# Hi and lo probabilities as one moving operand, and output parts summed by DRAM to DRAM transfers

## The chip, the cores and the metric

The kernel runs on one core of one Trainium2 chip. The metric is the device time of one execution in microseconds. TensorE multiplies matrices into PSUM, VectorE (DVE), ScalarE (ACT) and GpSimd (POOL) work on tiles, and SyncE (SP) issues the kernel's DMAs. The profile was taken from one execution; the runs were timed without it.

## What is computed

One layer of a streaming encoder in float32: 1024 frames of 1024 channels. Two attention groups of 8 heads each (64 channels per head) feed one output projection; then follow cross-attention into 256 memory rows and a squared-ReLU MLP. The part that the change touches is the token mixing:

```python
def forgetting_attention(q, k, v, f_logit):
    logf = jax.nn.log_sigmoid(f_logit.astype(jnp.float32))
    c = jnp.cumsum(logf, axis=1).transpose(0, 2, 1)
    for i in range(S // Q_BLOCK):
        ...
        logits = logits + c[:, :, q0:q1, None] - c[:, :, None, :q1]
        p = jax.nn.softmax(logits, axis=-1).astype(v.dtype)
        outs.append(jnp.einsum('bhqk,bkhd->bqhd', p, vb))

y = jnp.concatenate([rmsnorm(y_fox, g_fox_out), rmsnorm(y_chk, g_chk_out)], axis=-1)
x = x + rmsnorm(y @ w_out, g_mix_post)
```

The second group (chunked attention) sees its own chunk of 64 frames and the 8 before it, with a bias by relative position.

## The kernel before

**Precision by halves.** Matmuls run on float32r operands. To keep float32 accuracy each operand is kept as a hi half (rounded to float32r) and a lo half (the rest); a product is three matmuls, hi by hi, hi by lo and lo by hi (`mm3`, L172).

**Stages.** The first 80 us or so normalise the input and project the values of the first group. Then `attention_phase` (L1300) runs all attention together with the projections as filler; a second phase runs the output projection's second half and the memory attention; the MLP follows, written out by hand.

**The order of the work** in the attention phase is computed by a planner that runs when the kernel is built (`Flow`, L56). It holds a clock, a queue for each of VectorE ("V"), ScalarE ("S"), GpSimd ("G") and SP's DMA issues ("D"), and streams of TensorE steps (L1308): values, transposes, scores, side steps, and last the filler. At each moment it takes the first stream whose next step is ready by its own estimates. `flow.put(engine, at, cost, call, then, level)` places an operation with an estimated cost. Tokens (`free`, L235) count the buffers of each tag: `u4` counts free tiles of the large pool (34 tiles of 4 KB per partition, L153), from which the halves of the normalised input `hT` (16 tiles), the values `vs` (8), projected queries and keys, and other things are taken. The result is a fixed order of instructions for each engine; semaphores make each wait for its inputs.

**One head.** Scores of 128 queries are matmuls of up to 512 columns (L500, L501); VectorE adds the bias and keeps the minimum (L504), ScalarE takes the exponential (L513), VectorE the reciprocal of the sum (L515), GpSimd scales the probabilities (L516). In `turn_steps` (L556) TensorE transposes four 128 x 128 blocks of probabilities into a PSUM bank (L573): two key blocks by two query blocks. ScalarE copies them as the hi half `ph` (L582) and VectorE subtracts for the lo half `pl` (L579). A block that lies outside the mask is "dead" and left out: three blocks instead of four.

**Values times probabilities.** In `value_steps` (L588) a stationary tile of values holds 64 columns of hi and 64 of lo values of one head, so that one matmul (L613) gives v_hi·p on PSUM partitions 0 to 63 and v_lo·p on 64 to 127. Each step does four of them, `ph` and `pl` for each of two key blocks:

```python
todo = [(full, ph), (1 - full, ph), (1 - full, pl), (full, pl)]
```

A matmul moves 256 columns (two query blocks), or 128 where a block is dead. A unit is one head and one group of 256 queries; there are 64. At the end of a unit ScalarE copies the bank out (L622, 128 x 256), and SP stores the two partition halves to two DRAM tiles, `od[..][..]["h"]` and `["l"]` (L628).

**The outputs.** `Outputs.one` (L888) loads both halves of an output block of 128 channels by 512 frames (L929) for four blocks at a time, adds them (L920, on GpSimd for the first group and on VectorE for the second), scales and splits the sum (L921, L922) and takes the squares (L924, L899). The output projection of the first group (`mix_steps(0)`) comes at the end of the filler, then the memory values, then the second group's in the next phase.

**The gates.** `forget_gates` (L376) makes the logarithms of the gates; two groups of transposes (L401), two ScalarE copies (L405), a running sum on VectorE over 8 x 1024 (L409) and a store to DRAM (L411), from which each head's bias is loaded (L438). Its rows `ea`, `la`, `ua` live in tiles of the tag `klo`.

Of the kernel before, what the change touches and what calls it, by code (L numbers as in the profile page):

```python
# [14 lines left out]
F32 = mybir.dt.float32  # L15
F32R = mybir.dt.float32r
# [119 lines left out]
def build(ctx, tc, nc, out, t):  # L136
# [16 lines left out]
    def u4(name, shape, dt=F32R):  # L153

        return up.tile(list(shape), dt, tag="u4", bufs=34, name=name)
# [44 lines left out]
    od = [[[dr.tile([P, HT], F32, name=f"od{k}_{h}{m}") for m in "hl"] for h in range(2)] for k in range(KC)]  # L200
# [18 lines left out]
    def bias_rows(part):  # L219

        if part == 0:
# [14 lines left out]
            dict(s=2, tr=2, pv=2, mm=2, sp=5, p=2, klo=4, bias=2, raw=2, w=2, ot=3, u4=6,  # L236
# [139 lines left out]
    def forget_gates():  # L376

        z, e, l, u = [p1.tile([P, TB, 8], F32, tag="fg", bufs=4, name=f"f{n}") for n in "zelu"]
        ea, la, ua = [p1.tile([8, S], F32, tag="klo", bufs=4, name=f"f{n}a") for n in "elu"]
# [27 lines left out]
        def scan():  # L407
            vec.memset(ua, 0.0)
            vec.tensor_tensor_scan(la, ea, ua, 0.0, op0=ALU.add, op1=ALU.add)  # L409
# [146 lines left out]
    def turn_steps():  # L556
        for n, a, g in units:
            for c, (kbs, slots, dead) in enumerate(key_steps(n, g)):
# [8 lines left out]
                ph = p1.tile([P, 4, P], F32R, tag="ph", bufs=2, name=f"ph{nm}")  # L567
                pl = p1.tile([P, 4, P], F32R, tag="pl", bufs=2, name=f"pl{nm}")
# [15 lines left out]
                trs[n, a, g, c] = ph, pl  # L584
# [3 lines left out]
    def value_steps():  # L588
        landed = [all_of(("od", k), 32) for k in range(2)]
        for n, a, g in units:  # L590
# [4 lines left out]
            for c, (kbs, slots, dead) in enumerate(steps):  # L595
                yield (0.48, lambda: there(("t", n, a, g, c), ("v", n, 0), ("v", n, 1))
                       and (c or free["pv"].ready() and free["ot"].ready()))
                if c == 0:
                    free["pv"].take()
                    pv = mm_tile([P, 2, P], f"pv{n}{a}{g}", "pv")  # L600
                ph, pl = trs.pop((n, a, g, c))
                full = 1 if dead == [0] else 0
                todo = [(full, ph), (1 - full, ph), (1 - full, pl), (full, pl)]
                for m, (half, x) in enumerate(todo):
                    kb = kbs[slots[2 * half][0]]
                    if n < 4:
# [6 lines left out]
                    nc.tensor.matmul(pv[:, q0:q0 + k1 - k0, :], v, x[:, k0:k1, :], start=c == 0 and m == 0,  # L613
                                     stop=c + 1 == len(steps) and m == 3, skip_group_check=True)
                free["p"].give(flow.end)

            def leave(pv=pv, kind=kind, nm=f"{n}{a}{g}", a=a, kcol=kcol, g=g, step=1 if kind == "f" else -1):
                box = {}

                def copy():  # L620
                    box["t"] = p1.tile([P, 2, P], F32, tag="ot", bufs=3, name=f"ot{nm}")
                    nc.scalar.activation(box["t"][:, :, ::step], pv, AF.Copy)  # L622

                def store(at):
                    free["pv"].give(at)
                    done = all_of(("ot", nm), 2, lambda end: (free["ot"].give(end), landed["fc".index(kind)](end)))
# [97 lines left out]
    def side_steps():  # L724

        yield 0.87, lambda: flow.now > 10.0 and free["tr"].ready(2)
# [5 lines left out]
        def turned(at):  # L732
            for _ in range(2):
                free["tr"].give(at)
            flow.chain(at, [("V", 3.2, gate_scan), ("D", 0.55, gate_store)],
# [136 lines left out]
    class Outputs:  # L872
# [5 lines left out]
        def pump(self):  # L878
            while self.left:
                th, g = self.left[0]  # L880
                if not (there(("od", g)) and ((th, g) == (0, 0) or there("keys")) and free["u4"].ready(12 if (th, g) == (0, 0) else 9)):
                    break
                self.left.pop(0)
                for _ in range(9):
                    free["u4"].take()
                self.one(th, g)

        def one(self, th, g):  # L888
# [4 lines left out]
            ol = [u4(f"oil{th}{g}{i}", (P, 2, HT), F32) for i in range(2)]  # L893
            eng, add_cost, adder = ("G", 1.45, nc.gpsimd) if g == 0 else ("V", 0.7, nc.vector)
# [3 lines left out]
            def summed(at):  # L898
# [3 lines left out]
                def done(end):  # L902
                    seen["sq", th, g] = end
                    for _ in range(4):
                        free["u4"].give(end)
# [4 lines left out]
            for i in range(2):  # L910
                for j in range(2):
# [4 lines left out]
                    low = ol[i][:, j, :]  # L916

                    def loaded(at, gc=gc, o=o, dh=dh, dl=dl, dst=dst, low=low, last=i == 1 and j == 1):
                        flow.chain(at, [
                            (eng, add_cost, lambda: adder.tensor_add(o, o, low)),  # L920
# [6 lines left out]
                    here = all_of(("oin", th, kc), 2, loaded)  # L927
                    for m, x in enumerate((o, low)):
                        flow.load(flow.now, lambda x=x, kc=kc, m=m: nc.sync.dma_start(x, od[kc][th][m]), here, 3.0)  # L929
# [384 lines left out]
    with tc.manual_schedule():  # L1314
# [85 lines left out]
        def spread(th, d, tag):  # L1400
            ps = mm_tile([P, HT], f"rt{th}", tag)
            nc.tensor.matmul(ps, ones, d.rearrange("p a b -> p (a b)"), start=True, stop=True)
            r = p1.tile([P, HT], F32, tag="pl", bufs=2, name=f"rt{th}")
# [784 lines left out]
```

## Time and profile before

| | |
|---|---|
| median of 3 runs | 1488.19 us (1487.44 to 1494.37) |
| the profiled execution | 1486.78 us, its span 1485.0 us |
| mean granted TensorE clock | 0.997 |
| GpSimd busy, whole span | 378.1 us (25%) |
| DMA queue of SP | 238.18 MB, 46.8% of 16 engines' span |

A row of a timeline gives the start and duration in us, the engine, the line of the kernel, the operation, the tiles it writes and reads, its shape and the count of merged instructions. A row of a group gives the count, then busy time in us and mean duration in ns, then the idle time ahead of it and what ended it. Matmuls are pipelined: their durations overlap, so the distance between two starts is the time that one takes from TensorE. A row of a DMA group gives the count, the size, and the median time from issue to landing in us.

### The profile page before, as it was taken

To read this page: it belongs to the slowest core of one execution; us is meant where nothing else is said; L and a number is where in the kernel's file an instruction comes from. 1 tells how busy PE (TensorE), PEld (TensorE's weight loads), DVE (VectorE), ACT (ScalarE), POOL (GpSimd) and SP (SyncE) were. 2 spreads that over 40 slices of the span, in tenths; PEclk is the share of its full clock that TensorE was granted. 3 is DMA by queue.
4 is the path that set the end of the run, shared out by engine and by line. 5 is a ranking of instruction groups with operands and counts; after the bars stand their busy time and mean duration, and the time that the engine had idled before them with its cause. 6 is when DMAs were issued, how large, how long until landed. Compare 5 with 4: busy or idle time off the path is not lost. (4 is left out here: it accounts for less than half of the span.)

```text
span 1485.0 us, 21433 instructions
## 1 busy us (share of the span) xinstructions
PE 1462.4 (98%) x7564; PEld 1245.2 (84%) x7564; DVE 927.7 (62%) x1599; ACT 796.4 (54%) x1426; POOL 378.1 (25%) x464
## 2 busy tenths in 40 slices
PE   8899999999999999999999999999999999999998
PEld 7788888888889988888888887888888888888886
DVE  4857666466465654974374587675555665656577
ACT  7647666576566663563354454545555553443542
POOL 1334344335244310421031423432233000000021
PEclk9999999999999999999999999999999999999999
DMA  8033323424225568451241446764444685435475
GB/s 327 29 94 108 93 65 98 148 69 137 83 73 153 186 244 305 153 202 57 91 164 58 140 159 228 240 241 151 154 156 171 243 345 184 142 137 203 176 249 198
DMA packets 95355, 239.54 MB, mean 161 GB/s; under 512 B 11896, under 2 KB 20224, under 8 KB 95248
## 3 DMA queue, kind: packets, MB, share of 16 engines
q1 hardware_dynamic: 95248, 238.18, 46.8%
q8 instruction: 59, 0.97, 0.3%
q14 instruction: 48, 0.39, 0.1%
HBM read 170.45 MB, written 59.30 MB: 155 GB/s over the span
## 5 line engine op out<-in xcount | busy, mean ns | idle before, releaser
L579 DVE TENSOR_TENSOR pl<-ptr,ph 128x512 fp32r<-128x512 f32 (+1 forms) x152 | 92.4, 616 | 63.5 <-ACT ph L582 63.0
L582 ACT ACTIVATE ph<-ptr 128x512 fp32r<-128x512 f32 (+1 forms) x152 | 79.8, 540 | 48.5 <-PE ptr L573 45.9
L1912 ACT ACTIVATE whif<-ra 128x1024 fp32r<-128x1024 f32 x37 | 39.3, 1062 | 122.3 <-PE fy L175 62.6
L1914 DVE TENSOR_TENSOR wlof<-ra,whif 128x1024 fp32r<-128x1024 f32 x37 | 45.3, 1225 | 91.2 <-ACT whif L1912 91.1
L2028 POOL TENSOR_SCALAR rf<-sf 128x1 f32<-128x1 f32 x8 | 8.3, 1032 | 325.4 <-ACT jf L2013 325.1
L176 PE MATMUL fx<-vhif,wlof 128*128 128x512 f32 x168 | 65.4, 389 | 0.0
L175 PE MATMUL fx<-vlof,whif 128*128 128x512 f32 x168 | 65.4, 389 | 0.0
L174 PE MATMUL fx<-vhif,whif 128*128 128x512 f32 x168 | 65.4, 389 | 0.0
L613 PE MATMUL pv<-pl,vs 128*128 128x256 f32 (+1 forms) x304 | 64.6, 294 | 0.2 <-DVE pl L579 0.2
L613 PEld LDWEIGHTS pv<-ph,vs 128*128 128x128 f32 x304 | 53.1, 189 | 7.3
L613 PE MATMUL pv<-ph,vs 128*128 128x256 f32 (+1 forms) x304 | 58.1, 272 | 0.0
L1802 POOL TENSOR_TENSOR sc<-wf,wf 128x512 f32<-128x512 f32 x14 | 21.3, 1522 | 143.5 <-DMA wf<-in_w_ff 113.2
L174 PE MATMUL k<-hT_hi,whik 128*128 128x512 f32 x128 | 52.6, 411 | 0.0
L174 PE MATMUL q<-hT_hi,whiq 128*128 128x512 f32 x128 | 51.1, 399 | 1.3 <-DVE qs L703 1.3
L174 PE MATMUL mq<-h2T_hi,whimq 128*128 128x512 f32 x128 | 51.6, 403 | 0.0
L174 PE MATMUL yw<-whiwo,yT_hi 128*128 128x512 f32 x128 | 50.6, 396 | 0.4 <-ACT yt L1065 0.4
L174 PE MATMUL ym<-whimo,oT_hi 128*128 128x512 f32 x128 | 50.3, 394 | 0.1
L176 PE MATMUL k<-hT_hi,wlok 128*128 128x512 f32 x128 | 50.3, 393 | 0.0
L175 PE MATMUL k<-hT_lo,whik 128*128 128x512 f32 x128 | 50.3, 393 | 0.0
L176 PE MATMUL q<-hT_hi,wloq 128*128 128x512 f32 x128 | 50.1, 392 | 0.1
L175 PE MATMUL q<-hT_lo,whiq 128*128 128x512 f32 x128 | 50.1, 392 | 0.0
L175 PE MATMUL mq<-h2T_lo,whimq 128*128 128x512 f32 x128 | 50.0, 391 | 0.0
(597 smaller groups left out, 4979.7 us busy)
## 6 DMA issues: line engine op xcount, KB each, us to landing
ra<-gd SPq DMA_DIRECT2D x56, 512.0 KB, 3.5
wg<-in_w_ff SPq DMA_DIRECT2D x56, 512.0 KB, 4.9
wf<-in_w_ff SPq DMA_DIRECT2D x38, 512.0 KB, 3.9
gd<-s SPq DMA_DIRECT2D x48, 256.0 KB, 2.1
wrawmq<-in_w_mq SPq DMA_DIRECT2D x16, 512.0 KB, 3.8
wrawmo<-in_w_mo SPq DMA_DIRECT2D x16, 512.0 KB, 3.7
gd<-u SPq DMA_DIRECT2D x32, 256.0 KB, 2.1
gd<-g SPq DMA_DIRECT2D x25, 256.0 KB, 2.2
```

Source lines behind the costliest of these rows:

```text
L174: nc.tensor.matmul(ps, lh, rh, start=start, stop=False, skip_group_check=more)
L175: nc.tensor.matmul(ps, lh, rl, start=False, stop=False, skip_group_check=more)
L176: nc.tensor.matmul(ps, ll, rh, start=False, stop=stop, skip_group_check=more)
L579: flow.put("V", at, 0.56 if dead else 0.7, lambda: nc.vector.tensor_sub(pl[:, live, :], tr[:, live, :], f(ph[:, live, :])), done)
L582: flow.put("S", flow.end, 0.49 if dead else 0.6, lambda ph=ph, tr=tr, live=live: nc.scalar.activation(ph[:, live, :], tr[:, live, :], AF.C ...
L613: nc.tensor.matmul(pv[:, q0:q0 + k1 - k0, :], v, x[:, k0:k1, :], start=c == 0 and m == 0, stop=c + 1 == len(steps) and m == 3, skip_group_ ...
L1802: eng.tensor_sub(sc[:, k1], r0[:, k0], r1[:, k0])
L1912: nc.scalar.activation(ah, ra, AF.Copy)
L1914: nc.vector.tensor_sub(al, ra, f(ah))
L2028: nc.gpsimd.tensor_scalar(r, ssf[b][:, 0:1], ssf[b][:, 1:2], EPS, op0=ALU.add, op1=ALU.add)
```

## The change

Each step's `ph` and `pl` become the two halves of one tile `both`, and one matmul moves both: 512 columns, or 2 x 128 where a block is dead. The PSUM bank of a unit now holds two sums side by side, one of the hi and one of the lo probabilities, over hi and lo values as before. The copy out is 128 x 512. Three of its four parts are stored: v_hi·p_hi and v_hi·p_lo by one DMA, v_lo·p_hi by another; v_lo·p_lo is dropped. For each output block (8 by 2), when all eight stores have landed in the plan, GpSimd issues two DRAM to DRAM transfers with an accumulating add, one after the other, that add the second and third part onto the first. `Outputs` then loads one block instead of two and adds nothing; it waits for one half of the frames instead of both. The gates' rows move to tiles of the tag `bias`, and their running sum takes a minimum with its own input instead of an addition of zeros, so that the zeroed tile goes. The large pool has 32 tiles instead of 34, while the planner's count of free ones at the start of attention goes from 6 to 8. The scratch for GpSimd's DMA descriptors grows from 256 to 4096 bytes.

```diff
-        return up.tile(list(shape), dt, tag="u4", bufs=34, name=name)
+        return up.tile(list(shape), dt, tag="u4", bufs=32, name=name)
...
-    od = [[[dr.tile([P, HT], F32, name=f"od{k}_{h}{m}") for m in "hl"] for h in range(2)] for k in range(KC)]
+    od = [[dr.tile([3, P, HT], F32, name=f"od{k}_{h}") for h in range(2)] for k in range(KC)]
...
-            dict(s=2, tr=2, pv=2, mm=2, sp=5, p=2, klo=4, bias=2, raw=2, w=2, ot=3, u4=6,
+            dict(s=2, tr=2, pv=2, mm=2, sp=5, p=2, klo=4, bias=2, raw=2, w=2, ot=3, u4=8,
...
-        ea, la, ua = [p1.tile([8, S], F32, tag="klo", bufs=4, name=f"f{n}a") for n in "elu"]
+        ea, la = [p1.tile([8, S], F32, tag="bias", bufs=2, name=f"f{n}a") for n in "el"]
...
-            vec.memset(ua, 0.0)
-            vec.tensor_tensor_scan(la, ea, ua, 0.0, op0=ALU.add, op1=ALU.add)
+            vec.tensor_tensor_scan(la, ea, ea, 0.0, op0=ALU.add, op1=ALU.min)
...
-                ph = p1.tile([P, 4, P], F32R, tag="ph", bufs=2, name=f"ph{nm}")
-                pl = p1.tile([P, 4, P], F32R, tag="pl", bufs=2, name=f"pl{nm}")
+                both = p1.tile([P, 2, 4, P], F32R, tag="ph", bufs=2, name=f"p{nm}")
+                ph, pl = both[:, 0], both[:, 1]
...
+        landed = [[all_of(("od", g, th), 4) for th in range(2)] for g in range(2)]
+
+        def summed(kc, th):
+            def add(at, m=1):
+                if m == 3:
+                    return landed[kc // 4][th](at)
+                o = od[kc][th]
+                flow.put("G", at, 0.9, lambda: nc.gpsimd.dma_start(o[0], o[m], accum_op=ALU.add, max_dma_last_dim=2048),
+                         lambda end: add(end + 6.0, m + 1), 1)
+            return all_of(("ot", kc, th), 8, add)
+
+        sums = {(kc, th): summed(kc, th) for kc in range(KC) for th in range(2)}
...
-                yield (0.48, lambda: there(("t", n, a, g, c), ("v", n, 0), ("v", n, 1))
+                yield (0.35 if dead else 0.46, lambda: there(("t", n, a, g, c), ("v", n, 0), ("v", n, 1))
...
-                    pv = mm_tile([P, 2, P], f"pv{n}{a}{g}", "pv")
-                ph, pl = trs.pop((n, a, g, c))
+                    pv = mm_tile([P, 2, 2 * P], f"pv{n}{a}{g}", "pv")
+                x = trs.pop((n, a, g, c))
                 full = 1 if dead == [0] else 0
-                todo = [(full, ph), (1 - full, ph), (1 - full, pl), (full, pl)]
-                for m, (half, x) in enumerate(todo):
+                for m, half in enumerate((full, 1 - full)):
...
-                    nc.tensor.matmul(pv[:, q0:q0 + k1 - k0, :], v, x[:, k0:k1, :], start=c == 0 and m == 0,
-                                     stop=c + 1 == len(steps) and m == 3, skip_group_check=True)
+                    nc.tensor.matmul(pv[:, :, q0 * P:(q0 + k1 - k0) * P], v, x[:, :, k0:k1, :].rearrange("p m k q -> p m (k q)"),
+                                     start=c == 0 and m == 0, stop=c + 1 == len(steps) and m == 1, skip_group_check=True)
...
-                    box["t"] = p1.tile([P, 2, P], F32, tag="ot", bufs=3, name=f"ot{nm}")
-                    nc.scalar.activation(box["t"][:, :, ::step], pv, AF.Copy)
+                    box["t"] = p1.tile([P, 2, 2, P], F32, tag="ot", bufs=3, name=f"ot{nm}")
+                    nc.scalar.activation(box["t"][:, :, :, ::step], pv.rearrange("p m (k q) -> p m k q", q=P), AF.Copy)
...
-                    for m in range(2):
-                        flow.load(at, lambda m=m: nc.sync.dma_start(
-                            od[kcol][g // 2][m][a * 64:a * 64 + 64, (g % 2) * 256:(g % 2) * 256 + 256],
-                            box["t"][m * 64:m * 64 + 64].rearrange("p a b -> p (a b)")), done, 2.2)
+                    o = od[kcol][g // 2][:, a * 64:a * 64 + 64, (g % 2) * 256:(g % 2) * 256 + 256]
+                    flow.load(at, lambda: nc.sync.dma_start(
+                        o[0:2].rearrange("m p c -> p m c"), box["t"][0:64].rearrange("p m k q -> p m (k q)")), done, 2.2)
+                    flow.load(at, lambda: nc.sync.dma_start(
+                        o[2], box["t"][64:128, 0].rearrange("p k q -> p (k q)")), done, 2.2)
...
-                flow.put("S", flow.end, 0.4, copy, store)
+                flow.put("S", flow.end, 0.6, copy, store)
...
-        yield 0.87, lambda: flow.now > 10.0 and free["tr"].ready(2)
+        yield 0.87, lambda: flow.now > 13.0 and free["tr"].ready(2)
...
-                if not (there(("od", g)) and ((th, g) == (0, 0) or there("keys")) and free["u4"].ready(12 if (th, g) == (0, 0) else 9)):
+                if not (there(("od", g, th)) and ((th, g) == (0, 0) or there("keys")) and free["u4"].ready(13 if (th, g) == (0, 0) else 9)):
...
-            ol = [u4(f"oil{th}{g}{i}", (P, 2, HT), F32) for i in range(2)]
-            eng, add_cost, adder = ("G", 1.45, nc.gpsimd) if g == 0 else ("V", 0.7, nc.vector)
...
-                            (eng, add_cost, lambda: adder.tensor_add(o, o, low)),
...
-                    for m, x in enumerate((o, low)):
-                        flow.load(flow.now, lambda x=x, kc=kc, m=m: nc.sync.dma_start(x, od[kc][th][m]), here, 3.0)
+                    flow.load(flow.now, lambda o=o, src=od[kc][th]: nc.sync.dma_start(o, src[0]), loaded, 3.0)
...
-    nc = bacc.Bacc("TRN2", target_bir_lowering=False, num_devices=1, dynamic_dma_scratch_size=256)
+    nc = bacc.Bacc("TRN2", target_bir_lowering=False, num_devices=1, dynamic_dma_scratch_size=4096)
```

More of the change, by code (lines that the diff above doesn't have):

```diff
@@ L880, in pump @@
                 th, g = self.left[0]
-                if not (there(("od", g)) and ((th, g) == (0, 0) or there("keys")) and free["u4"].ready(12 if (th, g) == (0, 0) else 9)):
+                if not (there(("od", g, th)) and ((th, g) == (0, 0) or there("keys")) and free["u4"].ready(13 if (th, g) == (0, 0) else 9)):
                     break
                 self.left.pop(0)
-                for _ in range(9):
+                for _ in range(7):
                     free["u4"].take()
@@ L903, in done @@
                     seen["sq", th, g] = end
-                    for _ in range(4):
+                    for _ in range(2):
                         free["u4"].give(end)
@@ L914, in one, with loaded @@
                     dst = sq if kc % 4 == 0 else o
-                    low = ol[i][:, j, :]
-                    def loaded(at, gc=gc, o=o, dh=dh, dl=dl, dst=dst, low=low, last=i == 1 and j == 1):
+                    def loaded(at, gc=gc, o=o, dh=dh, dl=dl, dst=dst):
                         flow.chain(at, [
-                            (eng, add_cost, lambda: adder.tensor_add(o, o, low)),
                             ("S", 0.63, lambda: nc.scalar.activation(dh, o, AF.Copy, scale=gc)),
```

11 lines of the change are left out of this document (5 added, 6 removed).

## The prediction

> **What bounds the kernel now.** I read the engine table of the page first, then the table by stretches for the attention stage, then the waits of TensorE, then its timeline.
>
> ```profile
> span 1485.0 us, 21433 instructions
> ...
> PE 1462.4 (98%) x7564; PEld 1245.2 (84%) x7564; DVE 927.7 (62%) x1599; ACT 796.4 (54%) x1426; POOL 378.1 (25%) x464
> ```
>
> ```profile
> core 0: us, PE busy (x) PEld busy (x) DVE busy (x) ACT busy (x) POOL busy (x), PEclk, DMA share, GB/s
> 92.00:515.00 423.00, 422.49 (x2634) 376.41 (x2633) 266.78 (x759) 278.51 (x598) 174.52 (x257) 1.00 0.35 104
> ```
>
> ```profile
> PE yw L174 <- ACT yt L1065: 0.4, 1, 0.4
> ...
> PE sf0g L500 <- DVE mnf0g L504: 0.2, 1, 0.2
> ```
>
> TensorE is busy 1462 of 1485 us. In the stage that the change rewrites, 92 to 515 us, it is busy 422.5 of 423 at full granted clock, while VectorE stands at 63%, ScalarE at 66%, GpSimd at 41% and the DMA engines at 35%. The list of TensorE's waits between 95 and 620 us has four entries, of which the longest is 0.4 us. So an edit there is worth what it takes from or adds to TensorE's stream, and an edit elsewhere counts only when it makes TensorE wait. "Busy" overlaps for pipelined matmuls, so I price matmuls by the distance from one start to the next:
>
> ```profile
> 303.78 0.27 PE L500 MATMUL sc0g<-kd,qs 128*128 128x256 f32 x1
> 303.89 0.28 PE L501 MATMUL sc0g<-kl,qs 128*128 128x256 f32 x1
> 304.01 0.60 PE L573 MATMUL ptr<-ident,spc0g 128*128 128x128 f32 x4
> ...
> 304.92 0.39 PE L176 MATMUL q<-hT_hi,wloq 128*128 128x512 f32 x1
> 305.15 0.34 PE L613 MATMUL pv<-ph,vs 128*128 128x256 f32 x2
> 305.33 0.44 PE L613 MATMUL pv<-pl,vs 128*128 128x128 f32 x2
> 305.61 0.34 PE L500 MATMUL sc0g<-kd,qs 128*128 128x384 f32 x1
> ...
> 306.53 0.40 PE L613 MATMUL pv<-ph,vs 128*128 128x256 f32 x2
> 306.76 0.40 PE L613 MATMUL pv<-pl,vs 128*128 128x256 f32 x2
> 307.00 0.34 PE L500 MATMUL sc0g<-kd,qs 128*128 128x384 f32 x1
> ```
>
> A matmul of 512 columns takes 305.15 - 304.92 = 0.23 us, one of 256 takes (304.01 - 303.78) / 2 = 0.115. A value step with a dead block (256, 128, 128, 256 columns) takes 305.61 - 305.15 = 0.46 us; a whole one (four of 256) 307.00 - 306.53 = 0.47. A matmul of 128 columns is therefore not cheap: the two narrow ones of a dead step cost as much as two of 256. **That is the whole gain of the change.**
>
> **The change part by part.**
>
> *Value matmuls.* The forms give the number of steps of each kind:
>
> ```profile
> L613 PE MATMUL pv<-pl,vs x304: 272/283/337, 104.7 to 513.4; 128*128 128x128 f32 x80, 128*128 128x256 f32 x72
> ```
>
> 80 of the 152 steps have a dead block (one 128-wide lo matmul each), 72 have none. After the change a whole step is two matmuls of 512 columns: 2 x 0.23 = 0.46, 0.01 less. A dead step is one of 512 and one of 2 x 128 = 256 columns: 0.23 + 0.115 = 0.345, 0.115 less. Sum: 80 x 0.115 + 72 x 0.01 = 9.2 + 0.7 = **9.9 us less**. No moving operand or PSUM target in two separate pieces stands in the trace. If each piece cost as a matmul of its own today, a step would stay at 0.46 and the gain would be 0; that is one end. If two pieces of 128 ran like a 128-wide matmul whose weights are there already (305.15 to 305.33 is 0.115 + 0.065), the second matmul of a dead step would take 0.13 and the gain would be 8.7. At the full rate it is 9.9, the other end, since nothing in the rows is faster per column than 0.23 for 512. I take 9.9, from the rows of the same widths. All of it is on the path, since TensorE stops nowhere in the stage. The first matmul of a step now needs the lo half too, which the third needed so far, 0.23 us later; the planner releases a step only after the lo half, so I cost it at nothing; uncovered, it could cost at most 152 x 0.23 = 35 us, but only where VectorE runs behind the plan.
>
> *Copy out of the bank.* It doubles to 512 columns:
>
> ```profile
> L622 ACT ACTIVATE ot<-pv 128x256 f32<-128x256 f32 x63 | 23.9, 379 | 14.9 <-PE pv L613 14.4
> ```
>
> ```profile
> L582 ACT ACTIVATE ph<-ptr 128x512 fp32r<-128x512 f32 x72 | 42.6, 597 | 20.0 <-PE ptr L573 18.0 <-DVE pl L579 1.2
> ```
>
> 64 x (0.597 - 0.379) = 14 us more of ScalarE, 278.5 to 292 of 423 (69%), counted by the planner (0.6 for 0.4). Two pv banks and the filler matmuls hide it; cost 0.
>
> *What goes.* The gates' memset, and the adds of the two halves, eight on GpSimd and eight on VectorE:
>
> ```profile
> 75.90 0.91 DVE L408 MEMSET fua<- 8x1024 f32 x1 [0.16 <-issue]
> ```
>
> ```profile
> L920 POOL TENSOR_TENSOR oin<-oin,oil 128x512 f32<-128x512 f32 x6 | 8.1, 1355 | 17.6 <-DMA oil<-od_1l 11.0 <-DMA oil<-od_0l 6.6
> ```
>
> With them go 16 loads of 256 KB, while the stores stay two per unit. None of this ends a wait of TensorE: 0 us. The gates' step is planned 3 us later and its chain is 0.9 us shorter; the first scores need the key projection as well, and projections fill TensorE meanwhile: 0.
>
> *Sums by DMA.* There are 16 output blocks with two accumulating transfers each: 32 issues on GpSimd. The plan counts 0.9 us per issue, and lets the second follow 6.0 us after the first. Behind each in GpSimd's queue stand the probability scalings (L516), for which the transposes on TensorE wait. Such an issue does not occur in the trace. From below, the cheapest GpSimd operation of the stage takes 0.31 us; from above, I take the add that goes, 1.36:
>
> ```profile
> L462 POOL TENSOR_SCALAR_AFFINE_SELECT biasf<-biasf 128x128 f32<-128x128 f32 x59 | 18.3, 311 | 63.3 <-DVE mnf2g L504 7.7 <-DVE mnf5g L504 5.8 <-DVE mnf6g L504 5.4
> ```
>
> I choose 1.0, between them. How much lateness TensorE forgives shows in head f2, first and last group of its four:
>
> ```profile
> 141.91 1.02 POOL L516 TENSOR_SCALAR spf2g<-spf2g,smf2g 128x896 f32<-128x896 f32 x1
> ```
>
> ```profile
> 143.95 0.60 PE L573 MATMUL ptr<-ident,spf2g 128*128 128x128 f32 x4
> ```
>
> ```profile
> 155.92 0.38 POOL L516 TENSOR_SCALAR spf2g<-spf2g,smf2g 128x128 f32<-128x128 f32 x1 [0.81 <-DVE smf2g L515]
> ```
>
> ```profile
> 162.37 0.49 PE L573 MATMUL ptr<-ident,spf2g 128*128 128x128 f32 x3
> ```
>
> The first group is scaled at 142.93 and turned at 143.95, slack 1.0 us; the last at 156.30 and 162.37, slack 6.1. An issue that is 0.1 us over its planned 0.9 costs 32 x 0.1 = 3 us of GpSimd, of which a quarter, the groups with little slack, may reach TensorE: **0.8 us more**.
>
> How long an accumulating transfer of 256 KB takes is bounded by plain ones of that size:
>
> ```profile
> gd<-s SPq DMA_DIRECT2D x48, 256.0 KB, 2.1
> ...
> od_1h<-ot SPq DMA_DIRECT2D x32, 64.0 KB, 1.9
> ...
> oin<-od_0h SPq DMA_DIRECT2D x8, 256.0 KB, 5.3
> ```
>
> From below 2.1 us (a write alone), from above two reads and a write in series, 5.3 + 5.3 + 2.1 = 12.7. I take 5.3, the read of the same block, with write and second read beside it: under the planned 6.0, so GpSimd does not stand. The stores land in 1.9, and the plan allows 2.2.
>
> The Trainium skill ("DMA: Bandwidth & Descriptors", section "Anatomy of one DMA — SWDGE (gpsimd) path") fits a GpSimd transfer as about 2.0 us plus its bytes at 436 GB/s; an estimate from that page is 2.6 us here, and the sum would be the same. No run here shows such a transfer yet.
>
> *The end of the stage.* The sums put two transfers, some 13 us, between the last store and the loads of the second half of y. That half is ready and needed now at:
>
> ```profile
> L922 DVE SCALAR_TENSOR_TENSOR yT_lo<-oin,gcol,yT_hi x16: 743/752/1459, 345.5 to 543.5; 128x512 fp32r<-128x512 f32 x16
> ```
>
> ```profile
> 578.31 0.39 PE L174 MATMUL yw<-whiwo,yT_hi 128*128 128x512 f32 x1
> ```
>
> 543.5 against 578.3: 35 us of cover (the memory values run between), so 13 more cost 0. If that cover were gone, it would cost up to 13.
>
> *Sum against the profiled execution:* it took 1486.78 (span 1485.0 and 1.8 around it); 1486.8 - 9.9 + 0.8 = 1477.7. The three runs have a median of 1488.19, 1.4 above it, so I forecast **1479.1** for the median.
>
> **Rivals.**
>
> *Accumulates hold GpSimd (the slower side).* If a transfer takes L over 6.0 us, GpSimd stands w = L - 6.0 at each of the 16 second transfers. With slack spread evenly from 1 to 6 us, TensorE loses on average (w - 1)^2 / 10 each time. At L = 9.5 (w = 3.5) that is 16 x 0.62 = 10 us, which eats the gain; from L = 10.3 on the kernel is slower by over 0.5%; at L = 11 (w = 5) it is 26 us: 1479.1 + 25.6 = **1505**. For it: the upper bound of 12.7. Against it: DMA engines at 35%, and the 2.1 of a write.
>
> *More early tiles than there are.* At the start of attention 16 tiles of hT, 8 of values and 4 of weights are held: 34 - 28 = 6 was the planner's count; now 32 - 28 = 4 stand against a count of 8. Copies out of a projection may wait for a tile that the plan holds free. Price: one copy pair (0.6 on ScalarE, 0.69 on VectorE, the same size as L582) per pair of heads, 8 x 1.3 = 10.4: **1489**, no change. For it: the arithmetic. Against it: a projection takes its tokens some ten steps before its tiles.
>
> *The change does not do what it says.* Pieces cost as single matmuls: 1488.2 + 0.8 = **1489**.
>
> *Port lock.* VectorE could keep GpSimd from writing its descriptors, holding each issue by a VectorE operation of 0.69 us: 32 x 0.69 = 22 us of GpSimd, a quarter of it reaching TensorE, 5.5:
>
> ```profile
> L579 DVE TENSOR_TENSOR pl<-ptr,ph 128x512 fp32r<-128x512 f32 x72 | 49.4, 688 | 35.3 <-ACT ph L582 34.9
> ```
>
> That gives 1479.1 + 5.5 = **1485**. Against it: VectorE's large operations here read PSUM. The Trainium skill ("SBUF — State Buffer", section "SBUF: two separate sides") states this lock for VectorE operations in a 2-port mode, with 620 ns grown to 3100; the trace so far cannot show it.
>
> **How the numbers follow.** Forecast 0.66, with a range of its own of 1475.5 to 1482.5 (3.5 to either side, for the waits that a new order adds or removes); accumulates 0.18; early tiles 0.07; no saving 0.05; port lock 0.04. A measurement of this kernel can tell about 0.5% from no change, that is 7.4 us: faster is below 1480.7, slower above 1495.6. Since 1479.1 lies only 1.6 under that bound, the forecast gives 0.52 to faster and 0.14 to same. The accumulates give 0.08 to same and 0.10 to slower, early tiles 0.06 and 0.01, no saving 0.04 and 0.01, the port lock 0.04 to same. Sums: faster 0.52, same 0.36, slower 0.12. The new plan also reorders what comes behind attention, where TensorE still stands for 2.2 us:
>
> ```profile
> 520.00:760.00 240.00, 237.84 (x1159) 1.00 0.51 180
> ```
>
> The range begins at 1473: 1486.8 - 9.9, without the 0.8, less the waits of the stage (1.1) and these 2.2, with runs as low as the profile. It goes to 1494, which takes in early tiles, no saving and mild accumulates; left out are long accumulates and a little below.
>
> **What would show it.** Right: 224 value matmuls of 512 and 80 of 256 columns, 0.23 and 0.115 apart; TensorE's waits in the stage still about 1 us; the stage shorter by 9 to 10 us. Wrong: value steps still 0.46 apart where a block is dead; waits of TensorE's transposes on L516, with GpSimd standing at the second accumulate; copies out of projections that wait for a tile; an accumulate landing after more than 6 us.

## The result and the profile after

The changed kernel takes 1485.85 us in the median of 18 runs (1482.16 to 1488.96), the kernel before 1490.51 in 18 runs beside it: a ratio of 0.9968 with a 95% interval of 0.9959 to 0.9977, or 4.7 us less. Measured once more among the experiments it was 1487.72, a ratio of 0.9983 (0.9975 to 0.9991). The forecast was 1479.1, 9.1 us less than the median then known, so the sign was right and the size twice too large, by the second measurement (2.5 us by its ratio) over three times. The two profiled executions do not show even that: the one of before (1486.78) ran below all its timed runs, the one of after (1487.82) above its median. So I compare stretches inside the traces, not spans.

First the page of the changed kernel: TensorE has 4.7 us less, in 304 fewer matmul records.

```profile
span 1486.0 us, 20873 instructions
...
PE 1457.7 (98%) x7260; PEld 1228.0 (83%) x7260; DVE 921.0 (62%) x1590; ACT 804.0 (54%) x1426; POOL 387.4 (26%) x488
```

Then its attention stage by stretches, in the columns that the prediction shows for before.

```profile
92.00:515.00 423.00, 418.10 (x2349) 359.03 (x2348) 268.72 (x762) 288.23 (x602) 186.72 (x281) 1.00 0.51 129
```

ScalarE has 10 us more and DMA went from 35% to 51%, from the copies and the sums. But TensorE, which was busy for 422.5 of 423 us, now stands 4.9 us. Its groups by form and its timeline show that the value matmuls are what they were meant to be.

```profile
L622 PE MATMUL pv<-p,vs 128*128 128x512 f32 x224 | 76.9, 402 | 1.9 <-DVE p L578 1.9
L622 PE MATMUL pv<-p,vs 128*128 128x256 f32 x80 | 22.4, 280 | 0.0
```

```profile
306.36 0.52 PE L622 MATMUL pv<-p,vs 128*128 128x512 f32 x2
306.71 0.33 PE L499 MATMUL sc0g<-kd,qs 128*128 128x384 f32 x1
...
308.32 0.62 PE L622 MATMUL pv<-p,vs 128*128 128x512 f32 x2
308.78 0.33 PE L499 MATMUL sc0g<-kd,qs 128*128 128x384 f32 x1
```

A step with a dead block takes 306.71 - 306.36 = 0.35 us from its start to the next matmul (the row names the wider of its two forms), a whole one 0.46. Over all 152 steps the distances sum to 63.0 us, against 73.7 before: 10.7 less. So the saving is there, and half of it or more was lost elsewhere. The list of TensorE's waits over the whole span names the places.

```profile
PE q L174 <- DVE qs L714: 7.0, 1, 7.0
...
PE pv L622 <- DVE p L578: 1.9, 1, 1.9
PE ptr L572 <- POOL spc6g L515: 1.1, 1, 1.1
PE mk L176 <- POOL wlomk L320: 0.9, 1, 0.9
```

Before, the first was 1.3 us, beside a stop of 3.4 at the gates' transposes, and the others 0.2 or not there. The first is at the front of attention, the others at its back.

**The front.** TensorE's timeline before:

```profile
67.01 0.39 PE L176 MATMUL k<-hT_hi,wlok 128*128 128x512 f32 x1
70.77 1.86 PE L401 MATMUL ftr<-ident,fe 128*8 128x128 f32 x8 [3.37 <-DVE vs L1437]
72.28 0.77 PE L174 MATMUL k<-hT_hi,whik 128*128 128x512 f32 x1
...
75.17 0.47 PE L174 MATMUL q<-hT_hi,whiq 128*128 128x512 f32 x1 [1.26 <-DVE qs L703]
75.48 0.39 PE L175 MATMUL q<-hT_lo,whiq 128*128 128x512 f32 x1
```

and after:

```profile
68.84 0.39 PE L176 MATMUL k<-hT_hi,wlok 128*128 128x512 f32 x1
76.26 0.77 PE L174 MATMUL q<-hT_hi,whiq 128*128 128x512 f32 x1 [7.03 <-DVE qs L714]
76.83 0.63 PE L175 MATMUL q<-hT_lo,whiq 128*128 128x512 f32 x1
77.25 0.63 PE L176 MATMUL q<-hT_hi,wloq 128*128 128x512 f32 x1
...
80.24 1.58 PE L401 MATMUL ftr<-ident,fe 128*8 128x128 f32 x8
81.58 0.48 PE L174 MATMUL q<-hT_hi,whiq 128*128 128x512 f32 x1
```

In both, the second half of the query projection cannot start before VectorE has emptied the first one's bank (75.17 and 76.26: both 18.5 us after the first query matmul). Before, the gates' transposes and three key matmuls ran inside that stop. Now the stop is empty, and the transposes come after it. The changed kernel by stretches of 2 us has the granted clock in the third last column:

```profile
74.00:76.00 2.00, 0.00 (x0) 0.63 0.30 68
76.00:78.00 2.00, 1.74 (x4) 0.50 0.53 195
78.00:80.00 2.00, 2.00 (x6) 0.50 0.70 219
80.00:82.00 2.00, 2.00 (x12) 0.66 0.97 264
```

It is at half until about 81, so the projections stand 0.42 us apart (77.25 - 76.83) in place of 0.23. Before, the half clock had ended by 74, inside the stop:

```profile
70.00:72.00 2.00, 1.23 (x6) 0.59 0.00 0
72.00:74.00 2.00, 1.91 (x6) 0.56 0.00 0
74.00:76.00 2.00, 0.83 (x4) 1.00 0.73 246
```

The first score matmul comes 35.6 us after the first query matmul before (56.63 to 92.25), 39.6 after (57.77 to 97.33); 0.7 us of the difference is order alone, since three more query matmuls stand ahead of it.

**The back.** Around 460 us the queue of GpSimd in the changed kernel reads

```profile
451.38 0.81 POOL L595 DMA_DIRECT2D od<-od  x1 [4.22 <-DMA od<-od]
465.29 0.81 POOL L595 DMA_DIRECT2D od<-od  x1 [13.10 <-DMA od<-ot]
466.15 5.03 POOL L320 TENSOR_TENSOR wlomk<-wrawmk,whimk 128x512 fp32r<-128x512 f32 x4
471.16 0.37 POOL L515 TENSOR_SCALAR spc6g<-spc6g,smc6g 128x128 f32<-128x128 f32 x1
```

The accumulating transfer at 465.29 waits for a store of a head's output, and the weight splits and scalings behind it wait with it. ScalarE had what the first of those splits needs at 461.22 + 1.06 = 462.28, 3.9 us sooner than it ran:

```profile
461.22 1.06 ACT L311 ACTIVATE whimk<-wrawmk 128x1024 fp32r<-128x1024 f32 x1
```

The store was in good time in SyncE's queue, behind three weight loads:

```profile
454.34 0.53 SPq L298 DMA_DIRECT2D wrawmk<-in_w_mk  x1
...
457.20 1.05 SPq L298 DMA_DIRECT2D wrawmk<-in_w_mk  x2
458.34 0.62 SPq L638 DMA_DIRECT2D od<-ot  x1
```

and the trace has, for this store alone, who waited and how long it took to land:

```profile
  POOL od L595: 13.1, 1
...
DMA to landing us min/median/max: 6.5/6.5/6.5
```

6.5 us, where the plan has 2.2 and the median of its line is 2.4. In the second profile of the changed kernel this store landed in 4.7 us, but was issued at 460.4, and the splits ran 3.0 us late. That is the reading; the experiments test it.

### The profile page after: what moved, and what is told of

Its sections match the earlier page's. It is cut to its first block, busy times and chain, and to the rows that moved or that the text cites. A ratio compares the mean times of both kernels' runs of the same rounds, so it can differ in the third digit from the quotient of the medians.

```text
span 1486.0 us, 20873 instructions
## 1 busy us (share of the span) xinstructions
PE 1457.7 (98%) x7260; PEld 1228.0 (83%) x7260; DVE 921.0 (62%) x1590; ACT 804.0 (54%) x1426; POOL 387.4 (26%) x488
## 5 line engine op out<-in xcount | busy, mean ns | idle before, releaser
L578 DVE TENSOR_TENSOR p<-ptr,p 128x512 fp32r<-128x512 f32 (+1 forms) x152 | 92.3, 617 | 54.3 <-ACT p L581 53.6
L581 ACT ACTIVATE p<-ptr 128x512 fp32r<-128x512 f32 (+1 forms) x152 | 78.9, 539 | 39.9 <-PE ptr L572 39.0
L622 PE MATMUL pv<-p,vs 128*128 128x512 f32 (+1 forms) x304 | 85.9, 370 | 1.9 <-DVE p L578 1.9
L622 PEld LDWEIGHTS pv<-p,vs 128*128 128x128 f32 x304 | 55.0, 189 | 12.5 <-DVE p L578 2.3
L631 ACT ACTIVATE ot<-pv 128x512 f32<-128x512 f32 x64 | 38.0, 593 | 24.8 <-PE pv L622 23.2
L176 PE MATMUL yw<-whiwo,yT_lo 128*128 128x512 f32 x128 | 50.4, 394 | 0.0
L175 PE MATMUL yw<-wlowo,yT_hi 128*128 128x512 f32 x128 | 50.3, 393 | 0.0
```

Source lines behind the costliest of these rows:

```text
L175: nc.tensor.matmul(ps, lh, rl, start=False, stop=False, skip_group_check=more)
L176: nc.tensor.matmul(ps, ll, rh, start=False, stop=stop, skip_group_check=more)
L578: flow.put("V", at, 0.56 if dead else 0.7, lambda: nc.vector.tensor_sub(pl[:, live, :], tr[:, live, :], f(ph[:, live, :])), done)
L581: flow.put("S", flow.end, 0.49 if dead else 0.6, lambda ph=ph, tr=tr, live=live: nc.scalar.activation(ph[:, live, :], tr[:, live, :], AF.C ...
L622: nc.tensor.matmul(pv[:, :, q0 * P:(q0 + k1 - k0) * P], v, x[:, :, k0:k1, :].rearrange("p m k q -> p m (k q)"), start=c == 0 and m == 0, s ...
L631: nc.scalar.activation(box["t"][:, :, :, ::step], pv.rearrange("p m (k q) -> p m k q", q=P), AF.Copy)
```

## The experiments

Theory 1 puts the loss at the front (the gates' step), theory 2 at the accumulating transfers, theory 3 at early tiles that aren't there, theory 4 at the merge itself, since the work behind attention is not ready sooner. Two lengths of each trace tell them apart: from the first query matmul to the first score matmul (the front), and from the last matmul of the key projections to the last of the memory values (the back). What follows the back takes 905.9 to 907.5 us in every profile. What precedes the front varies: the first query matmul starts between 55.9 and 58.9 us, in no order of the kernels. Times are medians; ratios are to the kernel before beside them, and since the sets of runs come from different chips, kernels of different sets are better compared by ratio.

| kernel | us | ratio (95%) | front | back |
|---|---|---|---|---|
| before | 1489.5 to 1490.5 | 1 | 35.6 | 115.6 |
| changed | 1485.85 | 0.9968 (0.9959 to 0.9977) | 39.6 | 120.6 |
| changed, again | 1487.72 | 0.9983 (0.9975 to 0.9991) | 39.9 | 119.3 |
| gates_early | 1484.28 | 0.9959 (0.9944 to 0.9974) | 35.6 | 121.4 |
| sums_left_out | 1483.04 | 0.9958 (0.9944 to 0.9972) | 39.5 | 115.3 |
| tiles_4 | 1485.38 | 0.9974 (0.9963 to 0.9985) | 39.9 | 121.1 |
| merge_add | 1484.89 | 0.9969 (0.9957 to 0.9981) | 37.2 | 116.0 |
| sums_later | 1480.28 | 0.9935 (0.9923 to 0.9947) | 40.0 | 114.9 |
| sums_elsewhere | 1484.92 | 0.9963 (0.9951 to 0.9975) | 40.0 | 116.8 |
| both_put_right | 1479.28 | 0.9927 (0.9915 to 0.9940) | 35.6 | 113.9 |
| both_no_sums | 1477.07 | 0.9913 (0.9899 to 0.9926) | 37.9 | 113.2 |
| four_matmuls | 1488.36 | 0.9994 (0.9985 to 1.0003) | 36.9 | 115.9 |
| rows_later | 1476.79 | 0.9915 (0.9902 to 0.9929) | 34.7 | 113.0 |

**gates_early**: the gates' step back at its old place.

```diff
-        yield 0.87, lambda: flow.now > 13.0 and free["tr"].ready(2)
+        yield 0.87, lambda: flow.now > 10.0 and free["tr"].ready(2)
```

> The changed kernel with one number put back: the gates' step may come after 10.0 us of planned time again, not 13.0. Theory 1 (the later step makes TensorE stop once for 7.0 us instead of twice for 3.4 and 1.3, and its clock stays at half for 6.8 us instead of 3.4; with the gates' transposes that cost 3.9 us between 58 and 100 us): 3 to 4 us less than the changed kernel, about 1482, or 0.9943 of the kernel before; the profile has the transposes of the gates inside the stop and one clock row of 0.5 of 3.4 us there. Theory 2 (the loss comes from the accumulating transfers) and theory 3 (from early tiles): within 1 us of the changed kernel, 0.9968.

The front is 35.6 us again, 3.9 less, and TensorE's waits there are as long as before (the second is put down to ScalarE's copy of the gates here, to VectorE's `qs` before):

```profile
PE ftr L401 <- DVE vs L1441: 3.4, 1, 3.4
...
PE q L174 <- ACT fea L405: 1.2, 1, 1.2
```

The time fell by 1.6, and the intervals overlap, so the runs alone don't decide it; the stretch does, and it names what is not repaired: the back is as long as in the changed kernel.

**sums_left_out**: the accumulating transfers are not issued, their place in the plan stays.

```diff
-                flow.put("G", at, 0.9, lambda: nc.gpsimd.dma_start(o[0], o[m], accum_op=ALU.add, max_dma_last_dim=2048),
+                flow.put("G", at, 0.9, lambda: None,
```

> The changed kernel without its 32 accumulating transfers; the plan still counts 0.9 us and 6.0 us for each, so every other instruction stands where it stood. The outputs of the heads are then only the first of their three parts. Theory 2 (GpSimd's issues hold the scalings of the probabilities, or the transfers slow the others): 4 to 5 us less than the changed kernel, about 1481, or 0.994 of the kernel before. Theory 1 and the prediction (0.8 us for all 32): 0 to 1 us less, 0.996 to 0.997.

The back is 115.3, the value of before; theory 2 holds for this part, theory 1 for the front. The run is 2.8 us faster by medians, less than the 5.3 of the stretch, and the intervals of the ratios overlap: here too the stretch decides, not the time. GpSimd now starts the splits as soon as ScalarE has the first one's upper part, at 461.06 in this trace:

```profile
461.19 2.53 POOL L320 TENSOR_TENSOR wlomk<-wrawmk,whimk 128x512 fp32r<-128x512 f32 x2 [16.59 <-ACT whimk L311]
```

And the store lands no sooner: 7.0 us for the one issued at 456.7. It was late before anyone waited for it.

**tiles_4**: `u4=8` in the planner's counts is `u4=4`.

> The changed kernel with the planner's count of early tiles at 4, as many as there are, not 8. Theory 3 (copies out of projections wait for tiles that the plan holds free): 3 to 4 us less than the changed kernel, 0.994 of the kernel before. Theories 1 and 2: within 1.5 us of the changed kernel either way, 0.996 to 0.998, from a new order behind 300 us alone.

Nothing is gained, front and back stay. The rival of early tiles falls.

**merge_add**: the kernel before with the merge alone, and no sums by DMA.

```diff
...
-                    nc.scalar.activation(box["t"][:, :, ::step], pv, AF.Copy)
+                    nc.scalar.activation(box["t"][:, :, ::step], pv[:, 0].rearrange("p (k q) -> p k q", q=P), AF.Copy)
+
+                def both_sums(at):
+                    flow.put("V", at, 0.4, lambda: nc.vector.tensor_tensor(
+                        box["t"][:, :, ::step], box["t"][:, :, ::step], pv[:, 1].rearrange("p (k q) -> p k q", q=P), op=ALU.add), store)
...
```

Above this, the value matmuls are changed as in the change itself.

> The kernel before with the merged value matmuls alone: hi and lo probabilities as one moving operand, and on the way out of the bank ScalarE copies the first sum and VectorE adds the second (64 adds of 256 columns, planned 0.4 us each, 26 us of VectorE); two stores per unit, two loads and an add per block as before, gates as before, 33 tiles for 34. Theory 1 (the merge is worth its whole 10.7 us, and the rest of the change takes it back): 9 to 10 us less than the kernel before, 0.9935. Theory 4 (the merge itself gives back half, since the work behind attention isn't ready any earlier): 4 to 6 us less, 0.9965, with waits of TensorE behind 460 us as in the changed kernel. If VectorE's 26 us more reach TensorE: no faster than before.

4.6 us less, no more than the changed kernel gains, but for another reason: the back is 116.0, and the waits behind 460 us that theory 4 wanted are not there (none is over 0.7 us). It lost between: TensorE waits at scores for VectorE (1.3 us), which has 26.6 us of adds more, and 2.6 before the second query projection (1.3 before; that part I can't explain). So VectorE is no free place for the second sum, and the run doesn't measure the merge alone.

These four left one question: whether the transfers cost by waiting at the store, or by issue and traffic. The next four ran on one chip.

**sums_later**: GpSimd comes to a block's first transfer later.

```diff
-            return all_of(("ot", kc, th), 8, add)
+            return all_of(("ot", kc, th), 8, lambda at: add(at + 6.0))
```

> The changed kernel; the plan lets the first accumulating transfer of a block follow 6.0 us later after the planned landing of its last store, so that GpSimd doesn't come to it before the store has landed. Theory A (GpSimd stands at an accumulate whose store lands late, 6.5 us for a planned 2.2, and the weight splits and scalings queued behind it make TensorE wait and fall to half clock; worth 5 us between the last key projection and the end of the memory values, 120.6 in the changed kernel, 115.6 before): 115 to 116 us for that stretch, 4 to 5 us less in all, 1481, 0.994 of the kernel before. Theory B (the cost is the issues' own time, 32 of 0.86 us, or the transfers' share of the DMA engines): no change, 120 to 121 us for the stretch, 0.997.

Theory A: all 32 transfers are there, the back is 114.9, and the time is 1480.28, 7.4 us below the changed kernel beside it (the stretch accounts for 4 to 6 of them). GpSimd does the splits first:

```profile
462.99 2.55 POOL L320 TENSOR_TENSOR wlomk<-wrawmk,whimk 128x512 fp32r<-128x512 f32 x2 [10.19 <-ACT whimk L311]
467.88 1.30 POOL L320 TENSOR_TENSOR wlomk<-wrawmk,whimk 128x512 fp32r<-128x512 f32 x1 [2.34 <-ACT whimk L311]
469.12 0.80 POOL L595 DMA_DIRECT2D od<-od  x1
```

**sums_elsewhere**: the transfers stand where they stood, but go into blocks whose stores have landed.

```diff
-                o = od[kc][th]
-                flow.put("G", at, 0.9, lambda: nc.gpsimd.dma_start(o[0], o[m], accum_op=ALU.add, max_dma_last_dim=2048),
+                i = BLOCKS.index((kc, th))
+                k2, t2 = BLOCKS[i - m]
+                o = od[k2][t2]
+                flow.put("G", at, 0.9, lambda: i < m or nc.gpsimd.dma_start(o[0], o[m], accum_op=ALU.add, max_dma_last_dim=2048),
...
+        BLOCKS = [(kc, th) for kc in range(KC) for th in ((1, 0) if kc < 4 else (0, 1))]
```

> The changed kernel with each accumulating transfer at its place, of its size and with its issue, but into the block before (the second one: into the block before that), whose stores have long landed; so it waits for nothing. The sums of the outputs come out changed, and three of the 32 transfers are left out at the start. Theory A (waiting at the store): the stretch from the last key projection to the end of the memory values is 115 to 116 us, as with the transfers left out (115.3). Theory B (issues and traffic): 120 to 121 us, as in the changed kernel.

The back is 116.8, much nearer to theory A's 115 to 116 than to B's 120 to 121: issue and traffic without the wait keep about a quarter of the loss at most, 1.5 us over sums_left_out, hardly more than the 1.3 between the two profiles of the changed kernel. The time, 2.8 us below the changed kernel, is less than the stretch promises; this kernel has a wait of 1.3 us of the output projection on ScalarE (0.4 in the kernel before, none in the changed one), perhaps because loads of the outputs now stand behind transfers of later blocks. That is not settled.

**both_put_right**: both edits, `flow.now > 10.0` and `add(at + 6.0)`.

> The changed kernel with both edits: gates' step after 10.0 us again, first accumulates planned 6.0 us later. If both losses are what the two theories say, their parts add: 398 to 399 us from the first query projection to the last key projection (405.9 before, 401.8 in the changed kernel) and 115 to 116 us from there to the end of the memory values; 8 us less than the changed kernel in the sum of the two, 1478 to 1480, 0.9925 of the kernel before. If the losses are accidents of one order, which any new plan brings anew: no better than either edit alone, 0.995 to 0.997.

1479.28: 8.4 us below the changed kernel beside it, 10.4 below the kernel before. Front and back are both repaired at once (from the first query to the last key matmul it is 397.0 us, 1 to 2 better than expected), so the losses are two separate things and no accident of an order. Its attention stage leaves TensorE 0.6 us idle:

```profile
92.00:515.00 423.00, 422.44 (x2378) 364.11 (x2377) 272.00 (x766) 292.48 (x608) 191.01 (x281) 1.00 0.52 131
```

**changed_again**: the changed kernel beside these.

> The changed kernel once more, on the chip of the other three, so that they can be compared with it: 0.9968 of the kernel before, within the interval 0.9959 to 0.9977. Its profile shows which of its times repeat: by the theories the wait of 7.0 us before the second query projection, and 120 to 121 us from the last key projection to the end of the memory values; the start of the first query projection may vary (57.8 in the first profile, 56.3 to 58.3 in others).

Its ratio, 0.9983, is above the interval of the first measurement; its front and back repeat within 1.3 us.

**both_no_sums**: both edits, no transfers.

> The kernel with both edits (gates' step after 10.0, first accumulates 6.0 us later in the plan), without its 32 accumulating transfers; their places in the plan stay, and the outputs of the heads are the first of three parts. What the transfers cost where nobody waits at them: by the prediction's term 0.8 us (issues of 0.86 for a planned 0.9: rather 0), so 1478.5 to 1479.3, 0.992 to 0.9928 of the kernel before. If issues and traffic still cost TensorE time: 3 us or more below the kernel with both edits, 1476, 0.9905.

2.2 us less by medians, and the intervals of the ratios overlap: the transfers cost somewhere between nothing and some 5 us when nobody waits at them. The 0.8 of the prediction is neither confirmed nor excluded.

**four_matmuls**: both edits, but the value step in four pieces.

```diff
...
-                for m, half in enumerate((full, 1 - full)):
+                for half, m in ((full, 0), (1 - full, 0), (1 - full, 1), (full, 1)) if c else ((full, 0), (full, 1), (1 - full, 0), (1 - full, 1)):
...
-                    nc.tensor.matmul(pv[:, :, q0 * P:(q0 + k1 - k0) * P], v, x[:, :, k0:k1, :].rearrange("p m k q -> p m (k q)"),
-                                     start=c == 0 and m == 0, stop=c + 1 == len(steps) and m == 1, skip_group_check=True)
+                    nc.tensor.matmul(pv[:, m, q0 * P:(q0 + k1 - k0) * P], v, x[:, m, k0:k1, :].rearrange("p k q -> p (k q)"),
+                                     start=c == 0 and half == full, stop=c + 1 == len(steps) and (half, m) == (full if c else 1 - full, 1), skip_group_check=True)
```

> The kernel with both edits, but each value step again as four matmuls (hi and lo probabilities one after the other, each into its own half of the bank; planned at 0.48), everything else as it is. If the merged operand is what the change earns (10.7 us in the starts of the matmuls, 73.6 us for 152 steps before against 62.9 after): 10 to 11 us more than with both edits, 1489 to 1490.5, the time of the kernel before, ratio 0.9995 to 1.001. If the time comes from the rest of the change (sums by DMA, fewer adds and loads): 3 us or less more, 1482.

In this kernel each half of a bank has a start flag of its own in the first step, and its sums do not come out as those of the other kernels (most likely the second start drops what the first had summed; no run here shows how). The instructions and their sizes are those described.

```profile
L622 PE MATMUL pv<-p,vs 128*128 128x256 f32 x448 | 87.9, 291 | 0.0
L622 PE MATMUL pv<-p,vs 128*128 128x128 f32 x160 | 26.9, 250 | 0.0
```

1488.36, the time of the kernel before (its interval holds 1). So all the rest of the change, with both losses repaired, is worth nothing that can be told from zero; the merged operand is worth 9.1 us by medians, 0.9994 - 0.9927 = 0.0067 or 10.0 us by ratios, and 8.4 in the starts of the value matmuls of these two traces (71.4 against 63.0).

**rows_later**: both edits, and the bias rows behind the copies.

```diff
-        bias_rows(1)
-        flow.put("D", 14.0, 0.55, lambda: nc.sync.dma_start(rd, rows[0]))
-        flow.free.update(V=5.0, S=3.0)
+        flow.put("V", 13.5, 2.0, lambda: bias_rows(1), lambda at: flow.put(
+            "D", at, 0.55, lambda: nc.sync.dma_start(rd, rows[0])), 2)
+        flow.free.update(V=3.1, S=3.0)
```

> The kernel with both edits, and VectorE's three instructions on the bias rows (0.45, 0.06 and 1.39 us; needed for the second kind of heads alone) put behind the first projection's copies. If the stop of TensorE before attention ends with VectorE's queue, the wait of 1.2 us before the second query projection goes: 1 to 2 us less, 1477.5 to 1478.3, 0.9915 to 0.992. If it ends with ScalarE's copies of the gates: no change, 0.9927.

The wait before the second query projection fell from 1.2 to 0.4 us and the front to 34.7, as the first reading wants. From the first query to the last key matmul it is 397.0 us as without the edit, and the intervals of the times overlap. It is the fastest kernel here (1476.79); that it is faster than both_put_right is not shown.

## Where the prediction held and where it failed

Two steps of the sum failed. The gates' step was put at 0 and cost 3.3 us. The accumulating transfers were put at 0.8 and cost 4.7, by a wait for a late store, which the term took to be nothing. The other terms held.

*Value matmuls, -9.9.* Right: 10.7 less in the starts, 9.1 to 10.0 in the times. Two separate pieces run at the rate of one operand of their joint width (0.35 and 0.46 us for the two kinds of step); the end at which each piece costs as a matmul of its own, and the rival made of it, are out. That the first matmul of a step now needs the lo half was put at nothing. Near 514 us TensorE did stand for that half, 1.9 and 1.3 us in the two profiles of the changed kernel, but 0.1 and 0.6 in sums_elsewhere and sums_left_out, which have the same order, so this belongs to the loss at the back.

*Copies out of the bank, what goes, end of the stage.* Right. The copies take 593 ns (0.597 taken) and TensorE waits for none; of the 35 us of cover behind the memory values nothing shows as a wait of the output projection.

*The gates' step, "0".* Wrong, 3.3 us. "The first scores need the key projection as well, and projections fill TensorE meanwhile" was the argument. They can't fill it: they stood still themselves, for the bank that VectorE had to empty. The rows for this were in the profile of before (the stop of 3.37 us and the transposes right in it), and I didn't read which work TensorE had there. In six profiles with the late step the front takes 39.5 to 40.0 us, in the six with the early one and the old place of the bias rows 35.6 to 37.9, on average 36.5. It is no mere order: up to the last key matmul the six with the late step take 401.6 us on average, the three with the early step and otherwise the same change (gates_early, both_put_right, both_no_sums) 398.2.

*Accumulates, "0.8 us more".* Their issue was priced well (0.86 us, 1.0 taken) and so was the landing:

```profile
od<-od POOLq DMA_DIRECT2D x32, 256.0 KB, 4.5
```

4.5 against 5.3 taken and 6.0 planned. What failed is the sentence "The stores land in 1.9, and the plan allows 2.2": 1.9 is a median. The longest landing of such a store that can be read is 5.4 us in the trace of before and 8.3 in the changed one. A store that lands late cost nothing as long as no engine's queue stood on it. The change put GpSimd's queue on it, with splits and scalings behind. In the four profiles where GpSimd meets that store the back takes 119.3 to 121.4 us, in the eight where it doesn't (the kernel before among them) 113.0 to 116.0, and 116.8 in sums_elsewhere. With the four whose wait stands against the three before, merge_add and four_matmuls (115.6 to 116.0), that is 4.7 us on average.

*The rivals.* The slower side had the right engine and the wrong transfer: it made GpSimd stand at each of 16 second accumulates, for landings over 6.0. GpSimd did stand, idle, at six second ones and at five first ones, those for stores:

```profile
POOL od L595 <- DMA od<-ot: 26.8, 5, 13.1
POOL od L595 <- DMA od<-od: 24.6, 6, 5.5
```

But TensorE's list has only two waits for GpSimd in the whole span (1.1 and 0.9 us), both right behind the first accumulate at 465.29: one place decided. Port lock: issues took 0.79 to 1.13 us with VectorE at 64%, so no issue was held by 0.69. Early tiles: no effect in tiles_4.

*The sum.* 3.3 + 4.7 = 8.0 us of loss against 10.7 of saving leaves 2.7; measured were 4.7 and, the second time, 2.5 (ratio 0.9983). The traces alone show less than either: from the first query matmul to the last of the memory values it is 521.5 us before and 522.4 and 521.4 in the two profiles of the changed kernel, the whole saving gone. There is one trace of the kernel before, of an execution faster than its timed runs, so this difference stays open. With both steps put right the kernel takes 1479.28, 10.4 us below the kernel beside it, where the prediction had 9.1 with 0 and 0.8 for the two. That the measured 1485.85 lies inside the stated range, 1473 to 1494, is no merit of the sum: the range was made wide by other losses than the two that came.

## What to carry to other kernels

A DMA issued by a compute engine puts that engine's whole queue behind whatever the DMA waits for: price such a wait with the longest landing that the trace shows, in the stretch with most traffic, not with the median (here even the longest before, 5.4 us, was exceeded), or let the plan come to it later. Work that runs inside another wait is free only there; before it is moved, read what stands in that wait and what would run in its place. And a stop of TensorE can cost its length and then the clock.

## What the runs showed of the hardware

A store of 128 KB issued within 5 us behind three weight loads of 512 KB landed in 4.7 to 8.3 us in the nine profiles that have this order near 455 us, in place of 2.4 in the median; in the two of them without accumulating transfers it was 7.0 and 6.0.

After a stop of 1.9 us that began at 512.1 the granted clock of the changed kernel went to half for 3.4 us:

```profile
512.00:514.00 2.00, 0.10 (x1) 0.00 (x0) 1.88 (x3) 2.00 (x6) 0.00 (x0) 1.00 0.09 32
514.00:516.00 2.00, 1.99 (x9) 1.60 (x9) 0.69 (x1) 2.00 (x5) 0.84 (x1) 0.71 0.60 193
516.00:518.00 2.00, 2.00 (x7) 1.61 (x6) 1.16 (x2) 1.06 (x3) 0.00 (x0) 0.50 0.88 136
518.00:520.00 2.00, 2.00 (x10) 1.60 (x10) 1.38 (x2) 0.78 (x2) 0.32 (x1) 0.94 0.54 164
```

In the second profile the stop at the same place was 1.3 us, and the clock stayed at 1.00. The Trainium skill ("TensorE: Matmul & The Clock Gate", section "Part 1: The HAM clock gate") has the clock fall after at least one idle window of some 3.4 us; the length of the slow stretches agrees (3.4, and 6.8 behind the stop of 7.0), but here a stop of 1.9 us was enough.

An accumulating transfer of 256 KB from DRAM to DRAM landed in 3.7 to 7.1 us in the changed kernel, 4.5 in the median, and in up to 10.2 in the other kernels here; the estimate of 2.6 that the prediction made from the Trainium skill ("DMA: Bandwidth & Descriptors", section "Anatomy of one DMA — SWDGE (gpsimd) path") was too low for it.
